# One gathered block's gates and indices made per pair of heads, and its gathers issued from the first pair on

## The chip, the cores and the metric

The program runs on one core of a Trainium2 chip. The metric is device time in microseconds of one execution of the whole program, as the median of a few runs. The engines of the core are TensorE (PE), VectorE (DVE), ScalarE (ACT), GpSimd (POOL) and SyncE (SP, which issues most loads here); 16 DMA engines move the data between memory and the on-chip buffers.

## The reference

One transformer block in float32: 512 tokens of width 2048 pass a mixer (an mLSTM branch and a forgetting attention), then a cross attention to a memory, then a PEER feed-forward, each followed by a layer norm of 2^0.25 x + h. The part that matters here is the feed-forward: for each token and each of 8 heads, two lists of 128 scores are cut to their best 16, the best 16 of the sums are kept, and the 8 x 16 = 128 experts that they name are read from two tables of 16384 rows.

```python
q = (x @ w_pq).reshape(B, S, PEER_HEADS, 2, PEER_DK // 2)
sc = jnp.einsum('bshpd,hpnd->bshpn', q, sub_keys)
top_s, top_i = lax.top_k(sc, PEER_TOPK)
cand_s = (top_s[..., 0, :, None] + top_s[..., 1, None, :]).reshape(B, S, PEER_HEADS, 256)
best_s, best_pos = lax.top_k(cand_s, PEER_TOPK)
idx = jnp.take_along_axis(cand_i, best_pos, -1)   # cand_i = first index * 128 + second index
g = jax.nn.softmax(best_s, -1)
# per token t: a[k] = expert_u[idx[k]] . x[t];  out = sum_k gelu(a[k]) * g[k] * expert_v[idx[k]]
```

## The kernel before

The 512 tokens are four blocks of 128. Blocks 0 and 1 do the feed-forward by gathering: 128 jobs per block fetch one row of `peer_u` for each of the 128 tokens (an indirect DMA from POOL into a 128 x 2048 tile `rows`, L1062), and DVE multiplies it with the tokens and sums (L1082, the "u product"); 128 more jobs fetch rows of `peer_v`, which DVE adds with their weights (L1098, the "v product"). The tile `rows` has three buffers. Blocks 2 and 3 do it densely: all 16384 experts are multiplied on PE, with weights from `uT` and `vD`.

Every PE product is made from split operands. A 1 MB weight tile (`raw`) is loaded by SP (L168), ACT writes its rounded part into a `ring` tile (two copies of 128 x 1024, L194), DVE writes the rest (L199, "the split"), and PE multiplies with both. There are two wide ring tiles in the second half of the program. Each split calls `tick`, which adds `rate * cost * mult` to a credit and issues one job for each whole credit; the product of a job is placed some ticks later (`lag`).

The program is written in the order of its Python code, and a list scheduler then orders the instructions of each engine. That order is fixed when the program runs.

The order of the second half is this. Block 0's jobs run under the mixer of tokens 128 to 511. When they are used up, residuals, cross attention and norms follow for block 1 (one block of tokens, `nb` = 1) and for blocks 2 and 3 (`nb` = 2), interleaved by hand. In this stretch lies the stage `pick1` (L1313 to L1339): `Choice.run` multiplies block 1 with `peer_wq` in four groups, one for each pair of heads; after each group `select` cuts the scores of that pair (`MAX`, `MAX_INDEX`, `MATCH_REPLACE` on DVE: 16-wide lists) and writes two index parts `i0`, `i1` and the best scores. Behind the fourth pair `soften` makes the gates of all heads at once, and `indices(1)` makes the row numbers `ei[1]` and copies the gates into `gg[1]`. Then `add_jobs(1)` puts block 1's 256 jobs on the list, with a rate of 256 jobs over 980 units and `mult` 0.65. The stages behind are `topk` (the choice for blocks 2 and 3, `mult` 0.65), `gbuild` (their weights as a dense matrix, 1.5), and the dense multiplication with `uT` and `vD` (0.86). Block 1's last v product is followed by its layer norm (`fin_gathered`) and, at the end, those of blocks 2 and 3 (`fin`).

Which buffers a weight load may use depends on the job list, too. `load_raw` (L160) counts the loads since the list was used up; from the seventh on, every second load goes into a `rows` buffer, of which three are then free. With jobs on the list that doesn't happen, and only the two `raw` buffers of the pool `w` are left in this part of the program:

```python
raws["idle"] = raws["idle"] + 1 if jobs and state["done"] >= len(jobs) else 0
if raws["idle"] > 6 and raws["n"] % 2:
    raw = rows_tile("raw")
else:
    p = raws["pools"][raws["n"] % len(raws["pools"])]
    raw = p.tile([P, 2048], F32, tag="raw", bufs=1 if p is raws.get("one") else 2, name=nm("raw"))
```

## Time and profile before

| what | value |
|---|---|
| median of 3 runs | 4523.76 us (4520.47 to 4525.49) |
| the profiled execution | 4524.7 us, span 4523.0 us, granted clock 0.992 |
| busy share of the span | PE 98%, DVE 83%, ACT 49%, POOL 20% |
| DMA | 1491.85 MB, mean 330 GB/s |
| L1062, `peer_u` and `peer_v` gathers | 256 and 256 |
| L1082 u products, L1098 v products | 256 of 2285 ns, 256 of 2347 ns |

The span is the time from the first to the last instruction; the execution's own time is 1.7 us more. A row of the window view gives, for a stretch of the span in us, the busy time of PE, of PE's weight loads (PEld), DVE, ACT and POOL with their instruction counts, then the granted PE clock, the DMA engines' busy share and GB/s. A row of the waits gives the engine and line that waited, what ended the wait, the sum in us, the number of waits and the longest. In a row of instruction groups stand line, engine, operation, output and inputs, count, busy us and mean ns, and the idle time ahead of the group. A DMA row gives count, KB and the median time from issue to landing.

### The profile page before, as it was taken

What the parts mean: (1) busy time and instruction counts of PE and PEld (TensorE: products, weight loads), DVE (VectorE), ACT (ScalarE), POOL (GpSimd) and SP (SyncE); (2) the same over time, 40 slices, a digit from 0 to 9 for tenths busy, and PEclk for the clock granted to TensorE, in tenths of its full rate; (3) what the DMA queues carried; (4) which work ended last, traced back from release to release, by engine and by line L of the source; (5) the groups of instructions that cost most, each with busy time, mean ns of one, the idle gap of its engine ahead of it and who ended that gap; (6) DMA issues with size and microseconds to landing.
All of it is one profiled execution on the core that took longest, in us unless ns stands there. A gap on an engine that the chain in (4) does not pass through costs nothing.

```text
span 4523.0 us, 65247 instructions
## 1 busy us (share of the span) xinstructions
PE 4414.1 (98%) x25702; PEld 3966.6 (88%) x25702; DVE 3739.9 (83%) x4326; ACT 2229.8 (49%) x3032; POOL 895.5 (20%) x631
## 2 busy tenths in 40 slices
PE   9999999999999999999999999898999999999998
PEld 8888888889888899999999778898998778999996
DVE  7877768657898977888878778899988999888888
ACT  6876776645344422333333586543773444434443
POOL 1000000000132222232222000111222223334242
PEclk9999999999999999999999999999999999999999
DMA  8899989766798889898889866786999999999997
GB/s 311 317 334 337 335 320 336 271 233 217 280 336 342 330 335 347 336 344 318 325 337 350 296 246 236 284 319 243 366 352 422 414 415 408 378 391 391 378 360 302
DMA packets 246325, 1491.85 MB, mean 330 GB/s; under 512 B 26845, under 2 KB 54557, under 8 KB 77697
## 3 DMA queue, kind: packets, MB, share of 16 engines
q1 hardware_dynamic: 151680, 890.60, 52.3%
q0 software_dynamic: 81664, 561.95, 31.7%
q10 hardware_dynamic: 12672, 35.13, 2.0%
q8 instruction: 201, 3.29, 0.3%
q14 instruction: 108, 0.88, 0.1%
HBM read 1426.72 MB, written 60.86 MB: 329 GB/s over the span
## 4 chain that ended last, share of the span: by engine, by line
PE 65%; DVE 5%; issue 4%; DMA 3%; ACT 1%; POOL 1%; DVEq 0%; ACTq 0%; SPq 0%; POOLq 0%
PE mm L220 22%; PE mm L270 6%; PE mm L263 6%; PE mm L262 6%; PE pa L1381 4%; PE mm L1530 4%; PE mm L1531 4%; PE mm L1527 4%; PE pa L1374 4%; PE pa L1377 4%; DVE ring L199 2%; DMA raw<-in_vD 1%; POOL rows L1062 1%; PE sm L638 1%; PE sm L716 1%
## 5 line engine op out<-in xcount | busy, mean ns | idle before, releaser
L194 ACT CAST ring<-raw 128x1024 fp32r<-128x1024 f32 x1568 | 1597.0, 1051 | 1456.0 <-PE mm L220 479.4
L199 DVE TENSOR_TENSOR ring<-raw,ring 128x2048 fp32r<-128x2048 f32 (+1 forms) x926 | 1813.4, 1961 | 530.0 <-ACT ring L194 268.0
L1062 POOL DMA_INDIRECT rows<-in_peer_u,ei x256 | 377.2, 1474 | 1593.0 <-DVE rows L1082 767.3
L220 PE MATMUL mm<-Ah,ring 128*128 128x384 f32 x2560 | 667.5, 339 | 1.7 <-ACT c L674 1.7
L1062 POOL DMA_INDIRECT rows<-in_peer_v,ei x256 | 451.5, 1764 | 938.0 <-DVE x2l L1098 635.1
L1098 DVE SCALAR_TENSOR_TENSOR x2l<-rows,dots,x2l 128x2048 f32<-128x2048 f32 x256 | 600.8, 2347 | 7.5 <-DMA rows<-in_peer_v,ei 7.1
L1082 DVE SCALAR_TENSOR_TENSOR rows<-rows,x2l 128x2048 f32<-128x2048 f32 x256 | 584.1, 2285 | 19.1 <-DMA rows<-in_peer_u,ei 18.9
L1374 PE MATMUL pa<-Xh,ring 128*128 128x256 f32 x2048 | 489.2, 282 | 2.9 <-ACT ring L194 2.9
L1377 PE MATMUL pa<-Xl,ring 128*128 128x256 f32 x2048 | 486.4, 280 | 0.0
L220 PEld LDWEIGHTS mm<-Ah,ring 128*128 128x128 f32 x2560 | 461.5, 188 | 7.6 <-ACT c L674 2.1
L220 PE MATMUL mm<-Al,ring 128*128 128x384 f32 x1280 | 427.0, 337 | 0.0
L1530 PE MATMUL mm<-ring,hph 128*128 128x512 f32 x1024 | 400.2, 393 | 9.0 <-ACT ring L194 6.8
L1531 PE MATMUL mm<-ring,hpl 128*128 128x512 f32 x1024 | 397.9, 390 | 0.0
L1374 PEld LDWEIGHTS pa<-Xh,ring 128*128 128x128 f32 x2048 | 387.5, 189 | 6.6 <-ACT ring L194 4.1
L1377 PEld LDWEIGHTS pa<-Xl,ring 128*128 128x128 f32 x2048 | 387.3, 189 | 2.4
L262 PE MATMUL mm<-ring,Zh 128*128 128x512 f32 x832 | 326.6, 393 | 3.3 <-ACT ring L194 3.3
L263 PE MATMUL mm<-ring,Zl 128*128 128x512 f32 x832 | 325.6, 391 | 0.0
L262 PE MATMUL mm<-ring,Ah 128*128 128x512 f32 x768 | 303.8, 396 | 1.1 <-ACT ring L194 1.1
L263 PE MATMUL mm<-ring,Al 128*128 128x512 f32 x768 | 300.5, 391 | 0.0
L1381 PE MATMUL pa<-Xh,ring 128*128 128x256 f32 x2048 | 264.4, 282 | 2.5 <-DVE ring L199 2.4
L220 PE MATMUL mm<-Bh,ring 128*128 128x384 f32 x1024 | 262.4, 339 | 3.2 <-ACT ring L194 2.5
L1527 PE MATMUL mm<-ring,hph 128*128 128x512 f32 x1024 | 254.4, 390 | 5.2 <-DVE ring L199 5.2
(395 smaller groups left out, 7042.7 us busy)
## 6 DMA issues: line engine op xcount, KB each, us to landing
raw<-in_w_in SPq DMA_DIRECT2D x256, 1024.0 KB, 6.7
raw<-in_uT SPq DMA_DIRECT2D x128, 1024.0 KB, 9.1
raw<-in_vD SPq DMA_DIRECT2D x128, 1024.0 KB, 9.5
raw<-in_w_out SPq DMA_DIRECT2D x48, 1024.0 KB, 6.1
raw<-in_peer_wq SPq DMA_DIRECT2D x48, 1024.0 KB, 5.2
raw<-in_w_xkv SPq DMA_DIRECT2D x32, 1024.0 KB, 6.5
raw<-in_w_br_ml SPq DMA_DIRECT2D x32, 1024.0 KB, 6.8
raw<-in_w_br_fx SPq DMA_DIRECT2D x32, 1024.0 KB, 7.4
```

What stands on the lines that cost most here:

```text
L194: x = nc.scalar.copy(hi[:, c:c + 1024], src[:, c:c + 1024])
L199: s = nc.vector.tensor_sub(lo, src, hi.bitcast(F32))
L220: i = nc.tensor.matmul(o, w, x, start=start and s % per == 0, stop=stop and s % per == per - 1)
L262: nc.tensor.matmul(banks[t], xh[:, tt], wh[:, c], start=k == 0, stop=False)
L263: nc.tensor.matmul(banks[t], xl[:, tt], wh[:, c], start=False, stop=False)
L1062: i = nc.gpsimd.indirect_dma_start(out=rows, out_offset=None, in_=I[table], in_offset=bass.IndirectOffsetOnAxis(ap=ei[t][:, k:k + 1], axis=0))
L1082: i = nc.vector.scalar_tensor_tensor(rows, rows, 1.0, tok[t]["x2l"], op0=ALU.mult, op1=ALU.mult, accum_out=d[:, k % GB:k % GB + 1])
L1098: i = nc.vector.scalar_tensor_tensor(acc, rows, d[:, GB + k % GB:GB + k % GB + 1], acc, op0=ALU.mult, op1=ALU.add)
L1374: i = nc.tensor.matmul(bank, uh[:, sl], xh, start=k == 0, stop=False)
L1377: nc.tensor.matmul(bank, uh[:, sl], xl, start=False, stop=False)
L1530: nc.tensor.matmul(banks[t][g], a[:, tt], vh[:, gs_], start=c == c0, stop=False)
L1531: nc.tensor.matmul(banks[t][g], b[:, tt], vh[:, gs_], start=False, stop=False)
```

## The change

`settle(g)` is new. It is called behind each `select` of `pick1`, and makes that pair's gates (exponential on ACT; sum, reciprocal and product on DVE, straight into `gg[1]`) and that pair's 32 row numbers (`ep[g]`, two DVE instructions), then appends the pair's 32 u jobs to the list. `soften` and `indices(1)` are not called for block 1 any more. The credit, a rate of 256 over 980, a lag of 2 and `mult` 0.6 are set ahead of `pick1`. `add_jobs(1)` appends the 128 v jobs alone; it no longer resets the credit. The `mult` of the dense stage goes from 0.86 to 0.81. Order and number of the 256 gathers of the block are the same.

```diff
+            def settle(self, g):
+                sl = slice(32 * g, 32 * g + 32)
+                e = self.gates[:, 0, sl]
+                ev = e.rearrange("p (h k) -> p h k", k=16)
+                sm = self.tp.tile([P, 2], F32, tag="s", bufs=2, name=nm("s"))
+                nc.scalar.activation(e, e, AF.Exp)
+                nc.vector.tensor_reduce(out=sm, in_=ev, axis=AX.X, op=ALU.add)
+                nc.vector.reciprocal(sm, sm)
+                nc.vector.tensor_tensor(gg[1][:, sl].rearrange("p (h k) -> p h k", k=16), ev,
+                                        sm.unsqueeze(2).to_broadcast([P, 2, 16]), op=ALU.mult)
+                ef = self.tp.tile([P, 32], F32, tag="ef", bufs=2, name=nm("ef"))
+                nc.vector.scalar_tensor_tensor(ef, self.sel["i0"][0][:, sl], float(PKEYS), self.sel["i1"][0][:, sl],
+                                               op0=ALU.mult, op1=ALU.add)
+                nc.vector.tensor_copy(ep[g], ef)
+                jobs.extend((job_u, 1, k) for k in range(32 * g, 32 * g + 32))
...
                         self.select(t, 2 * g, sc)
-                self.soften()
+                        if settle:
+                            self.settle(g)
+                if not settle:
+                    self.soften()
...
-                                             in_offset=bass.IndirectOffsetOnAxis(ap=ei[t][:, k:k + 1], axis=0))
+                                             in_offset=bass.IndirectOffsetOnAxis(
+                                                 ap=ep[k // 32][:, k % 32:k % 32 + 1] if t else ei[0][:, k:k + 1], axis=0))
...
-            jobs.extend((f, t, k) for f in (job_u, job_v) for k in range(NC_))
+            jobs.extend((f, t, k) for f in (job_u, job_v)[t:] for k in range(NC_))
...
             c = Choice(pp, pp, 1)
-            cr = c.run(X2b, nc.sync)
+            state["lag"], state["rate"], state["credit"], state["mult"] = 2, 2 * NC_ / 980.0, 0.0, 0.6
+            cr = c.run(X2b, nc.sync, True)
...
-            c.indices(1)
...
         add_jobs(1)
-        state["lag"] = 2
-        set_rate(980.0)
         state["mult"] = 0.65
...
-        state["mult"] = 0.86
+        state["mult"] = 0.81
```

The scheduler's order changes with it. Line numbers of the changed program are its own: L169 is the load, L200 the split, L1104 the u product, L1120 the v product; the instructions of `select` stand one line lower. Numbers in names tell tiles of the same kind apart. The first place is SP's queue around the load of the second pair's weights. Before:

```order
L168 DMA raw_21665<-in_peer_wq 128x2048
L168 DMA raw_21830<-in_peer_wq 128x2048
L168 DMA raw_21735<-Ad 128x2048
L168 DMA raw_21864<-in_peer_wq 128x2048
L168 DMA raw_21847<-in_peer_wq 128x2048
L168 DMA raw_21914<-Ad 128x2048
L1012 DMA keysT_21628<-in_keysT 128x512
L1012 DMA keysT_21827<-in_keysT 128x512
L1069 DMA x2l_22923<-x2d 128x2048
L168 DMA raw_21881<-in_peer_wq 128x2048
```

Now:

```order
L169 DMA raw_21668<-in_peer_wq 128x2048
L169 DMA raw_21738<-Ad 128x2048
L169 DMA raw_21841<-in_peer_wq 128x2048
L1030 DMA keysT_21631<-in_keysT 128x512
L1030 DMA keysT_21838<-in_keysT 128x512
L1091 DMA x2l_21846<-x2d 128x2048
L169 DMA raw_21864<-in_peer_wq 128x2048
L169 DMA raw_21881<-in_peer_wq 128x2048
L169 DMA raw_21901<-in_peer_wq 128x2048
L1030 DMA keysT_22036<-in_keysT 128x512
```

Before, three of the second pair's four weight loads stood ahead of the two key loads and the block's `x2l` load; now one does, and three stand behind them.

The second place is DVE from the split with which the last of the cross attention's `Ad` tiles is taken (the 14th split counted from the one at 2717.10 us of the profile). Before:

```order
L199 TENSOR_TENSOR ring_149<-raw_22122,ring_149 128x2048
L946 MATCH_REPLACE rep_21959<-v_21943,sc_21912 128x128
L946 MATCH_REPLACE rep_21965<-v_21943,sc_21912 128x128
L982 SCALAR_TENSOR_TENSOR pp_21811<-pf_21813,pp_21811 128x32
L989 TENSOR_TENSOR eq_21818<-eq_21818,ixf_21790 128x512
L199 TENSOR_TENSOR ring_19990<-raw_22196,ring_19990 128x2048
L947 MAX v_21943<-rep_21959 128x8
L947 MAX v_21943<-rep_21965 128x8
L983 TENSOR_TENSOR pf_21813<-pp_21811 128x32
L990 TENSOR_REDUCE sel_i_2363_21625<-eq_21818 128x32
```

Now:

```order
L200 TENSOR_TENSOR ring_152<-raw_22158,ring_152 128x2048
L977 TENSOR_SCALAR pos_21997<-pos_21997 128x32 x2
L1014 TENSOR_REDUCE s_22028<-sel_g_21630 128x2
L1104 SCALAR_TENSOR_TENSOR rows_21848,dots_21886<-rows_21848,x2l_21846 128x2048
L979 CAST pp_22012<-pos_21997 128x96
L1015 RECIPROCAL s_22028<-s_22028 128x2
L1104 SCALAR_TENSOR_TENSOR rows_21850,dots_21886<-rows_21850,x2l_21846 128x2048
L981 SCALAR_TENSOR_TENSOR pf_22014<-pp_22012 128x32
L1016 TENSOR_TENSOR gg_147<-sel_g_21630,s_22028 128x32
L942 MAX v_22264<-sc_22125 128x8 x4
L1104 SCALAR_TENSOR_TENSOR rows_21939,dots_21886<-rows_21939,x2l_21846 128x2048
```

At the same split the first pair's selection was still under way before; now it is finished, the second pair's is at its end (32 more DVE instructions stand ahead of this split than before), and the first three u products of block 1 stand directly behind the split. Twelve u products stand between it and the 27th split, where before none did; from there until the split at 3775 us of the profile the changed order is 12 to 15 products ahead of the old one at the same split. In the 66 splits from 3388 to 3775 us the old order holds 66 products and the new one 65; behind them the lead falls from 14 to two or three at the end.

The third place is DVE at the end of the program. Before, the block's last v product and the statistics and first half of its layer norm stood behind the last split, and the second half stood among the last norms of blocks 2 and 3. Now:

```order
L200 TENSOR_TENSOR ring_152<-raw_37362,ring_152 128x2048
L1120 SCALAR_TENSOR_TENSOR x2l_21846<-rows_37273,dots_30439,x2l_21846 128x2048
L1150 BN_STATS fst_37420<-x2l_21846 128x6 x4
L1151 BN_AGGR fst_37420<-fst_37420 128x2
L1132 SCALAR_TENSOR_TENSOR x2l_21846<-x2l_21846,fst_37420,lw_37358 128x1024 x2
L287 TENSOR_SCALAR fst_37420<-fst_37420 128x1
L200 TENSOR_TENSOR ring_19993<-raw_37391,ring_19993 128x2048
L289 RECIPROCAL fst_37420<-fst_37420 128x1
```

The norm's first half now stands ahead of the last but one split, and its second half ahead of the last one.

More of the change, by code (lines that the diff above doesn't have):

```diff
@@ L133, in build @@
         iota = cp.tile([P, P], F32, tag="iota", name="iota")
-        ei = [cp.tile([P, P], I32, tag=f"ei{t}", name=f"ei{t}") for t in range(2)]
+        ei = [cp.tile([P, P], I32, tag="ei0", name="ei0")]
         nc.gpsimd.iota(ei[0], pattern=[[1, P]], base=0, channel_multiplier=0)
@@ L150, in build @@
         gg = [cp.tile([P, P], F32, tag=f"gg{t}", name=f"gg{t}") for t in range(2)]
+        ep = [cp.tile([P, 32], I32, tag=f"ep{g}", name=f"ep{g}") for g in range(4)]
         ticks = []
@@ L1004, in soften, with run @@
                 nc.vector.tensor_tensor(e, e, sm.unsqueeze(2).to_broadcast([P, 8 * nb, 16]), op=ALU.mult)
-            def run(self, X2, ld):
+            def settle(self, g):
[13 more added lines that the diff above has]
+                jobs.extend((job_u, 1, k) for k in range(32 * g, 32 * g + 32))
+            def run(self, X2, ld, settle=False):
                 tp, nb = self.tp, self.nb
@@ L1314, in build @@
             c = Choice(pp, pp, 1)
-            cr = c.run(X2b, nc.sync)
+            if state["done"] < len(jobs):
+                raise RuntimeError(f"{len(jobs) - state['done']} jobs left")
+            state["lag"], state["rate"], state["credit"], state["mult"] = 2, 2 * NC_ / 980.0, 0.0, 0.6
+            cr = c.run(X2b, nc.sync, True)
             for i in range(15):
@@ L1338, in build @@
             next(cr, 0)
-            c.indices(1)
         pre = ExitStack()
         pp = pre.enter_context(pool("pre", side="right"))
-        while state["done"] < len(jobs):
-            raise RuntimeError(f"{len(jobs) - state['done']} jobs left")
         add_jobs(1)
-        state["lag"] = 2
-        set_rate(980.0)
         state["mult"] = 0.65
```

## The prediction

> **What bounds the kernel now.** I read the page's head, then the windows by stage, then who waits in the stretch that the change touches.
>
> ```profile
> span 4523.0 us, 65247 instructions
> PE 4414.1 (98%) x25702; PEld 3966.6 (88%) x25702; DVE 3739.9 (83%) x4326; ACT 2229.8 (49%) x3032; POOL 895.5 (20%) x631
> ```
>
> TensorE is busy nearly everywhere, so the question for each stage is how much PE idles there, and for whom. The windows of the stages behind `pick1`:
>
> ```profile
> 2880.00:3120.00 240.00, 239.12 (x2032) 238.71 (x2031) 228.48 (x524) 101.33 (x116) 40.35 (x29) 1.00 0.83 320
> 3160.00:3420.00 260.00, 252.41 (x2127) 249.11 (x2125) 234.10 (x239) 183.06 (x453) 66.81 (x40) 0.99 0.93 365
> 3420.00:3785.00 365.00, 351.30 (x1617) 285.17 (x1616) 339.04 (x288) 145.51 (x169) 98.31 (x64) 1.00 1.01 415
> 3785.00:4455.00 670.00, 667.65 (x4286) 608.12 (x4285) 584.57 (x326) 274.65 (x303) 251.32 (x116) 1.00 0.96 382
> ```
>
> From 3785 us on, where the change has about 12 gathers fewer, PE is busy 667.65 of 670 us: no more than 2.35 us can be won there. From 3420 to 3785 us the DMA engines are full (share 1.01), PE idles 13.7 us, and that is where fewer gathers would help; but the order places 66 products in those 66 splits before and 65 now. From 2880 to 3120 us PE is busy 239.12 of 240, so whatever is late at 2880 stays late.
>
> Now `pick1` and the norm behind it, from the 1st to the 14th split after 2717 us, to the 27th, and to the next stage's first split:
>
> ```profile
> 2717.00:2768.70 51.70, 49.67 (x228) 40.38 (x227) 43.52 (x97) 37.13 (x50) 0.00 (x0) 0.97 0.83 311
> 2768.70:2836.00 67.30, 62.92 (x286) 51.43 (x284) 65.89 (x160) 31.67 (x43) 0.00 (x0) 1.00 0.42 149
> 2836.00:2867.30 31.30, 22.95 (x136) 18.87 (x137) 22.53 (x86) 24.00 (x44) 0.00 (x0) 0.78 0.44 156
> 2717.00:2867.30 150.30, 135.54 (x648) 110.68 (x647) 131.95 (x341) 92.80 (x136) 0.00 (x0) 0.94 0.56 206
> ```
>
> POOL does nothing here and the DMA engines are at 0.56, which is what the change means to use. But in the middle stretch DVE is busy 65.89 of 67.30 us. DVE is the bound there, and PE follows it: PE loses 4.4 us in the middle and 8.4 behind. What DVE waits for in its idle 8.2, 1.4 and 8.8 us:
>
> ```profile
> DVE ring L199 <- ACT ring L194: 9.5, 6, 3.1
> DVE v L941 <- ACT sc L1040: 6.1, 2, 5.5
> DVE ring L199 <- PE mm L220: 5.5, 2, 3.4
> ```
>
> The 5.5 us wait is the last stretch's: the fourth pair's scores, which nothing but PE and ACT can hurry.
>
> **The change part by part.** The costs per instruction, from the groups:
>
> ```profile
> L1082 DVE SCALAR_TENSOR_TENSOR rows<-rows,x2l 128x2048 f32<-128x2048 f32 x256 | 584.1, 2285 | 19.1 <-DMA rows<-in_peer_u,ei 18.9
> L976 DVE TENSOR_SCALAR pos<-pos 128x32 uint32<-128x32 uint32 x8 | 1.0, 173 | 0.0
> L199 DVE TENSOR_TENSOR ring<-raw,ring 128x2048 fp32r<-128x2048 f32 x27 | 61.7, 2286 | 9.8 <-ACT ring L194 8.3 <-PE mm L270 1.5
> L194 ACT CAST ring<-raw 128x1024 fp32r<-128x1024 f32 x55 | 55.7, 1053 | 43.6 <-DVE ring L199 20.7 <-PE mm L263 19.2 <-DVE xst L861 2.5
> ```
>
> *Moved and added DVE work.* By the order twelve u products now stand between the 14th and the 27th split: 12 x 2.285 = 27.4 us. `settle` makes 4 x 5 DVE instructions in place of six, 14 more; the nearest row is one of 32 wide at 173 ns: 2.4 us. Together 29.8 us. The old idle can take in some of it. The order puts 32 more of the short selection instructions (0.17 to 0.29 us, some 8 us) ahead of the 14th split, where 8.2 us are idle. So the middle holds 65.89 + 29.8 - 8 = 87.7 us of work against 67.30 us before: +20.4 us even if DVE there never waits. The last stretch keeps its wait for the scores, which comes behind the moved products: 0. The floor, with all 18.35 us of idle filled, is 29.8 - 18.35 = +11.4 us; the ceiling, with none filled, +29.8.
>
> *Buffers for the loads.* With jobs on the list from the first `settle` on, `load_raw` stops giving out `rows` tiles. So the weight loads fall from five buffers (two of `w`, three of `rows`) to two, just where the matrices for one block take a new tile every few us. SP's queue shows it: two more of the second pair's weights now queue behind the key and `x2l` loads.
>
> ```profile
> raw<-in_peer_wq SPq DMA_DIRECT2D x18, 1024.0 KB, 5.5
> raw<-in_w_in SPq DMA_DIRECT2D x93, 1024.0 KB, 7.1
> 2733.74 2.29 DVE L199 TENSOR_TENSOR ring<-raw,ring 128x2048 fp32r<-128x2048 f32 x1 [0.22 <-PE mm L270]
> 2768.71 2.29 DVE L199 TENSOR_TENSOR ring<-raw,ring 128x2048 fp32r<-128x2048 f32 x1
> ```
>
> One buffer's round is the landing (5.5 us here; 7.1 in the stage at 1300 to 2400 us, which runs gathers with two buffers), two ACT copies (2.1) and the split (2.3): 9.9 to 11.5 us, so two buffers give a split each 4.95 to 5.75 us. Between the two quoted splits lie nine intervals in 35.0 us. At 4.95 they take 44.6, at 5.75 51.8: +9.6 to +16.8 us, and the 8 us of earlier selection fit inside. I take +11, near the row of this stretch. The low end is 0, if the loads are asked for early enough. In the middle, 13 intervals in some 88 us are 6.7 us each, over the 4.95: the loads bind only where two splits stand close.
>
> *Gathers that land late.* DVE runs in order, so a product whose rows have not landed holds up the splits queued behind it, and PE waits for those.
>
> ```profile
> rows<-in_peer_u,ei POOLq DMA_INDIRECT x71, 9.8
> 3906.04 2.75 POOL L1062 DMA_INDIRECT rows<-in_peer_v,ei  x1 [4.96 <-DVE x2l L1098]
> 3911.11 1.14 POOL L1062 DMA_INDIRECT rows<-in_peer_v,ei  x1 [2.32 <-DVE x2l L1098]
> ```
>
> In the next stage (2880 to 3420 us) a gather lands 9.8 us after its issue. By the order some two dozen short instructions and two splits, about 9 us, lie between the first pair's row numbers and the first product, and three gathers of 1 MB start together there. I take +5 us for this and for close splits in the middle, from 0 (all hidden) to 18 (a 1.5 us wait at each of twelve products). The Trainium skill's page "DMA: Bandwidth & Descriptors", section "Anatomy of one DMA — SWDGE (gpsimd) path", gives a DMA from POOL about 2.0 us plus its bytes over 436 GB/s, an estimated 4.4 us for 1 MB; by that every gather would be hidden and the sum 5 us less. The 9.8 us of the row are more than twice that.
>
> *Behind `pick1`.* Between 3160 and 3388 us the lead grows from 12 to 15, three more products and 3 MB where the DMA share is 0.93: 0 to 3 x 2.285 = 6.9 us; I take 2, as DVE still idles 26 us in that window. The lower `mult` has no price.
>
> *The end.*
>
> ```profile
> 4499.42 1.97 PE L1527 MATMUL mm<-ring,hph 128*128 128x512 f32 x8
> 4511.15 2.48 DVE L1113 SCALAR_TENSOR_TENSOR x2l<-x2l,fst,lw 128x1024 f32<-128x1024 f32 x2
> ```
>
> PE's last product ends at 4501.4; behind it DVE alone sets the end. The second half of the gathered block's norm, 2.48 us, now stands ahead of the last split: -2.5 us, from -5 (with its small steps) to +3 (if it makes the last splits late).
>
> **Sum** on the profiled execution's 4524.7 us (0.9 over the median, nothing here): 11 + 20.4 + 5 + 2 - 2.5 = +35.9, so **4561 us**.
>
> **The rivals.** *VectorE alone:* the loads are asked for early and gathers land in time; then the first stretch costs nothing: 20.4 + 2 - 2.5 = +19.9, 4545 us. For it: DMA share 0.56. Against it: five buffers become two. *The idle absorbs it:* every idle us of DVE is filled, +11.4 - 2.5, 4534 us. Against it: 8.8 of the 18.35 us lie behind the last moved product. *Not slower:* the relief at the end pays. Place: 3785 to 4455 us. Price: 12 gathers of 1.05 MB at the 382 GB/s of that window, 33 us, which would give 4561 - 33 = 4528, and 4501 together with the floor. It decides if PE waits for gathers or loads there, and the window's 2.35 us of idle speak against it. *Gathers that start slowly:* in the dense stage, where DVE is nearly full, a gather takes POOL 2.75 us in one row and 1.14 in the next. If each of the twelve starts 1.6 us late with DVE full and DVE waits for each, that is +19 more: 4580 us. Beside it stands a rule of the Trainium skill, page "SBUF — State Buffer", section "Who interferes with whom": a VectorE instruction with two inputs in that memory blocks a GpSimd instruction that reads it, and the splits and products are such. The two lengths in the trace fit it; against a price POOL's idle 150 us speak, since a late start only counts if the landing does. *That the change does not do what it says,* the order excludes: the products stand where the text puts them.
>
> **How the numbers follow.** A measurement here tells about 0.2% (9 us) from no change. Forecast 0.50; VectorE alone 0.25; slow gathers 0.10; absorbed 0.08; relief at the end 0.07. The range is 4533 to 4586: down to the absorbed case, and up to the sum with the loads at 16.8 and the gathers at 18 (4580), plus 6 of the 10 us that the growing lead (4.9) and the end (5.5) could add at their worst. Faster by over 0.2% needs the relief together with the floor: 0.05. Within 0.2%: 0.02 of the relief and 0.05 of the absorbed case, whose 4534 lies on the edge: 0.07. Slower: the rest, 0.88.
>
> **What would show it.** In the profile after: `rows` products from about 2780 us on; the 14th split some 11 us later, the 27th some 36 us later; DVE busy nearly all of the time between them; weight loads that are issued only when a split has freed a buffer, and DVE waits for L194's line that end in a `raw` landing; PE idle of 40 us or more in this stretch; from there the same stages shifted by one amount, and an end some 2 us shorter. If the 27th split comes at its old time, the reckoning of DVE's work is wrong; if the shift is 20, that of the buffers; if the dense stage from 3785 us is shorter by more than 3 us, that of the end.

## The result, and the profile after

The changed kernel takes 4557.84 us in the median of four runs (4550.52 to 4564.33), the kernel before 4523.74 beside it: a ratio of 1.0076, 95% interval 1.0064 to 1.0088. It is slower by 34.1 us, where 37 were forecast. The profiled execution took 4558.29 us. The head of its page:

```profile
span 4556.6 us, 65269 instructions
PE 4421.1 (97%) x25702; PEld 3966.0 (87%) x25702; DVE 3741.9 (82%) x4340; ACT 2231.2 (49%) x3037; POOL 884.3 (19%) x631
```

VectorE's busy time grew by 2.0 us and PE's by 7.0, with the same number of matmuls; the rest of the 33.6 us by which the span grew is waiting. Work was moved, hardly any added. Where the time lies is read by cutting both executions at the same splits: the 1st, 14th and 27th of the prediction, the next stage's first, and the 16th from the end. The windows of before, with the row that sums the three of `pick1` and the norm, then the two behind:

```profile
sum 150.18, PE 135.42 PEld 110.56 DVE 131.92 ACT 92.67 POOL 0.00; mean PE 45.14 PEld 36.85 DVE 43.97 ACT 30.89 POOL 0.00
...
2867.27:4408.30 1541.03, 1499.59 (x10047) 1374.54 (x10046) 1393.79 (x1478) 705.06 (x1054) 450.02 (x243) 0.99 0.93 372
4408.30:4523.00 114.70, 92.06 (x469) 78.19 (x467) 100.71 (x89) 34.47 (x38) 30.12 (x13) 0.93 0.77 302
```

And of after, at the same splits (the cuts of a run lie up to 0.4 us ahead of its splits, all by the same amount, 0.16 us here; so the differences between cuts hold, and "the end" is that much too long):

```profile
2720.12:2783.66 63.54, 54.36 (x232) 40.82 (x231) 51.41 (x138) 35.35 (x50) 4.26 (x3) 0.95 0.66 240
2783.66:2873.14 89.48, 67.87 (x282) 53.05 (x280) 85.60 (x158) 36.19 (x50) 13.52 (x11) 0.91 0.77 286
2873.14:2904.33 31.19, 22.73 (x131) 18.68 (x132) 22.17 (x85) 23.74 (x43) 0.00 (x0) 0.72 0.52 182
sum 184.21, PE 144.96 PEld 112.55 DVE 159.17 ACT 95.28 POOL 17.79; mean PE 48.32 PEld 37.52 DVE 53.06 ACT 31.76 POOL 5.93
...
2904.33:4442.04 1537.71, 1494.01 (x10054) 1372.20 (x10053) 1374.76 (x1456) 704.55 (x1054) 432.37 (x233) 0.99 0.92 366
4442.04:4556.60 114.56, 92.37 (x465) 77.54 (x463) 94.69 (x85) 34.13 (x38) 21.08 (x11) 0.94 0.71 279
```

The first split comes at 2720.28 us instead of 2717.10: 3.2 us that this execution had lost by then; executions differ by as much (in e5 below, the same program, it comes at 2713.7). Then the first stretch grows by 11.9 us (51.61 in the kernel before, from its 2717.09 to 2768.70), the middle by 22.1 (67.36 before), the last by nothing: `pick1` takes 184.2 us instead of 150.2, 34.0 more. Behind it 3.3 us are won, at the end no more than 0.3. In the middle stretch VectorE is busy 85.60 of 89.48 us, as before it was 65.9 of 67.4: it is still the bound, with 19.7 us more to do; 2.5 us more of idle make up the 22.1.

Who waits in `pick1`, on VectorE and then on TensorE:

```profile
DVE ring L200 <- ACT ring L195: 13.1, 8, 6.5
DVE v L942 <- ACT sc L1058: 5.5, 1, 5.5
...
DVE rows L1104 <- DMA rows<-in_peer_u,ep: 2.6, 2, 2.0
```

```profile
PE mm L271 <- DVE ring L200: 17.1, 6, 11.0
PE mm L263 <- ACT ring L195: 12.0, 7, 5.6
```

These rows are of 2715 to 2905 us. The splits' wait for ACT's copy alone tells little: in the kernel before it is 8.3 us within the stretch (the 9.5 quoted in the prediction are of 2707 to 2880 us). What ACT's copies themselves wait for has changed. Before (2717 to 2867 us), then after (2720 to 2904 us):

```profile
ACT ring L194 <- DVE ring L199: 20.7, 5, 7.2
ACT ring L194 <- PE mm L263: 19.2, 15, 6.0
```

```profile
ACT ring L195 <- DMA raw<-in_peer_wq: 31.1, 10, 6.3
ACT ring L195 <- DMA raw<-Bd: 22.4, 6, 10.2
```

Before, ACT waited for VectorE and PE, and for weight tiles to land 1.0 us in all; now it waits 59.8 us for landings (the third row, of `Ad`, is 6.3): the loads bind. The wait for the fourth pair's scores is the old 5.5 us, to the tenth. Only two products waited for their gathers, 2.6 us together, but what stood behind them waited too. PE waits 17.1 us for splits, 11.0 of it for the 27th alone, which VectorE, with its queue of selection and products, reaches only at 2873. On SP's queue, in time order with start and length:

```profile
2722.60 0.33 SPq L169 DMA_DIRECT2D raw<-in_peer_wq  x1
2729.05 0.80 SPq L1030 DMA_DIRECT2D keysT<-in_keysT  x2
2729.95 0.38 SPq L1091 DMA_DIRECT2D x2l<-x2d  x1
2731.61 0.33 SPq L169 DMA_DIRECT2D raw<-in_peer_wq  x1
```

For 9 us after 2722.60 no weight tile is asked for; in the kernel before, five are asked for from 2719.42 to 2736.07, never more than 5.4 us apart. The tile asked for at 2731.61 holds up the split that needs it:

```profile
2742.04 2.29 DVE L200 TENSOR_TENSOR ring<-raw,ring 128x2048 fp32r<-128x2048 f32 x1 [6.51 <-ACT ring L195]
```

It starts 8.8 us after the split ahead of it, where before it was 2.5.

### The profile page after: what moved, and what is told of

Same layout as the page of the kernel before. It is cut to its first block, busy times and chain, and to the rows that moved or that the text cites. A ratio compares the mean times of both kernels' runs of the same rounds, so it can differ in the third digit from the quotient of the medians.

```text
span 4556.6 us, 65269 instructions
## 1 busy us (share of the span) xinstructions
PE 4421.1 (97%) x25702; PEld 3966.0 (87%) x25702; DVE 3741.9 (82%) x4340; ACT 2231.2 (49%) x3037; POOL 884.3 (19%) x631
## 4 chain that ended last, share of the span: by engine, by line
PE 57%; DMA 7%; DVE 6%; issue 6%; ACT 2%; POOL 1%; DVEq 0%; ACTq 0%; SPq 0%; POOLq 0%
PE mm L221 22%; PE mm L271 5%; PE mm L264 5%; PE mm L263 5%; DMA rows<-in_peer_v,ep 3%; PE pa L1401 3%; PE pa L1394 3%; PE pa L1397 3%; DVE ring L200 2%; PE mm L1547 2%; PE mm L1550 2%; PE mm L1551 2%; DMA raw<-in_vD 1%; POOL rows L1083 1%; ACT ring L195 1%
## 5 line engine op out<-in xcount | busy, mean ns | idle before, releaser
L200 DVE TENSOR_TENSOR ring<-raw,ring 128x2048 fp32r<-128x2048 f32 (+1 forms) x926 | 1811.2, 1960 | 552.8 <-ACT ring L195 286.1
L1120 DVE SCALAR_TENSOR_TENSOR x2l<-rows,dots,x2l 128x2048 f32<-128x2048 f32 x256 | 600.4, 2345 | 21.7 <-DMA rows<-in_peer_v,ep 18.4
L1104 DVE SCALAR_TENSOR_TENSOR rows<-rows,x2l 128x2048 f32<-128x2048 f32 x256 | 583.4, 2283 | 13.6 <-DMA rows<-in_peer_u,ei 7.7
L1394 PE MATMUL pa<-Xh,ring 128*128 128x256 f32 x2048 | 489.0, 282 | 5.1 <-ACT ring L195 5.0
L1550 PE MATMUL mm<-ring,hph 128*128 128x512 f32 x1024 | 399.9, 392 | 7.5 <-ACT ring L195 5.7
L1083 POOL DMA_INDIRECT rows<-in_peer_u,ep x128 | 192.2, 1501 | 1036.4 <-DVE rows L1104 401.3
L1083 POOL DMA_INDIRECT rows<-in_peer_v,ep x128 | 279.1, 2180 | 539.0 <-DVE x2l L1120 299.0
L1083 POOL DMA_INDIRECT rows<-in_peer_u,ei x128 | 173.2, 1353 | 516.6 <-DVE rows L1104 316.1
L1083 POOL DMA_INDIRECT rows<-in_peer_v,ei x128 | 173.1, 1353 | 474.1 <-DVE x2l L1120 261.1
```

The costliest lines, as they stand in the source:

```text
L200: s = nc.vector.tensor_sub(lo, src, hi.bitcast(F32))
L1083: i = nc.gpsimd.indirect_dma_start(out=rows, out_offset=None, in_=I[table], in_offset=bass.IndirectOffsetOnAxis(ap=ep[k // 32][:, k % 32:k ...
L1104: i = nc.vector.scalar_tensor_tensor(rows, rows, 1.0, tok[t]["x2l"], op0=ALU.mult, op1=ALU.mult, accum_out=d[:, k % GB:k % GB + 1])
L1120: i = nc.vector.scalar_tensor_tensor(acc, rows, d[:, GB + k % GB:GB + k % GB + 1], acc, op0=ALU.mult, op1=ALU.add)
L1394: i = nc.tensor.matmul(bank, uh[:, sl], xh, start=k == 0, stop=False)
L1550: nc.tensor.matmul(banks[t][g], a[:, tt], vh[:, gs_], start=c == c0, stop=False)
```

## The experiments

Each kernel ran beside the kernel before on one chip; "the stretch" is `pick1` from the first split to the next stage's first, 150.2 us in the kernel before. In four runs that move no products, gathers or buffers in it (e6, e8, e9, e11) it takes 150.0 to 150.5, and in the three profiles of the changed kernel's own order (after, e5, e10) 184.2 to 185.7; so a difference of 2 us is seen there, while whole executions of the kernel before lay up to 24 us apart (4510.67 to 4534.77, beside e1). All of it in one table; "behind" runs from the next stage's first split to the 16th from the end, "end" from there to the last instruction, all from the profiled executions:

| run | stretch | against before | behind | end | ratio of the times (95%) |
|---|---|---|---|---|---|
| before | 150.2 | | 1541.0 | 114.7 | |
| after | 184.2 | +34.0 | 1537.7 | 114.6 | 1.0076 (1.0064 to 1.0088) |
| e1: two load buffers alone | 159.7 | +9.5 | 1533.9 | 115.0 | 1.0020 (1.0007 to 1.0033) |
| e2: after, no products | 169.6 | +19.4 | 1551.8 | 114.9 | 1.0081 (1.0060 to 1.0103) |
| e3: after, no gathers | 179.8 | +29.6 | 1550.9 | 118.1 | 1.0094 (1.0071 to 1.0118) |
| e4: after, three buffers | 174.0 | (17 late at its start) | 1550.7 | 116.2 | 1.0115 (1.0094 to 1.0137) |
| e5: after again | 185.7 | +35.5 | 1538.3 | 116.1 | 1.0079 (1.0064 to 1.0093) |
| e6: settle alone | 150.5 | +0.3 | 1546.3 | 115.2 | 1.0020 (1.0010 to 1.0030) |
| e7: products alone | 170.2 | +20.0 | 1538.2 | 116.3 | 1.0055 (1.0040 to 1.0069) |
| e8: before, 0.94 | 150.0 | -0.2 | 1543.6 | 128.8 | 1.0046 (1.0033 to 1.0059) |
| e9: before, 0.90 | 150.0 | -0.2 | 1544.2 | 112.9 | 1.0000 (0.9991 to 1.0009) |
| e10: after, 0.86 | 184.4 | +34.2 | 1544.3 | 108.2 | 1.0053 (1.0038 to 1.0069) |
| e11: before, 12 gathers fewer | 150.4 | +0.2 | 1535.8 | 109.1 | 0.9985 (0.9975 to 0.9994) |
| e12: after, half the rate | 171.7 | +21.5 | 1552.2 | 114.7 | 1.0070 (1.0054 to 1.0085) |

**e1, two load buffers alone.** The kernel before, with

```diff
-            raws["idle"] = raws["idle"] + 1 if jobs and state["done"] >= len(jobs) else 0
+            raws["idle"] = raws["idle"] + 1 if jobs and not raws.get("hold") and state["done"] >= len(jobs) else 0
...
                         self.select(t, 2 * g, sc)
+                        raws["hold"] = nb == 1 and not self.lean
...
         add_jobs(1)
+        raws["hold"] = False
```

> The kernel before, with one thing changed: from the first selection of pick1 on, the weight loads get no rows tiles, so two buffers instead of five; no settle, no earlier gathers. My theory (the loads' two buffers cost the first stretch its 12 us, VectorE's moved products the middle its 22): the 14th split comes 10 to 13 us later than in the kernel before, the 27th split keeps that shift or gives up to 5 us of it back, since VectorE without the moved products has little idle there; time about 4534 (4529 to 4537), 7 to 13 over the kernel before. Rival (the loads are asked for early enough, and the first stretch became longer through settle and the new order of the selection): 14th split within 3 us of its old time, time 4522 to 4527.

The three windows of its stretch:

```profile
2714.45:2778.81 64.36, 55.08 (x230) 42.05 (x229) 51.31 (x135) 35.30 (x48) 0.00 (x0) 0.92 0.63 221
2778.81:2847.50 68.69, 64.38 (x287) 51.92 (x285) 60.97 (x127) 36.12 (x49) 0.00 (x0) 1.00 0.55 198
2847.50:2874.17 26.67, 20.94 (x132) 17.77 (x133) 20.61 (x81) 20.89 (x40) 0.00 (x0) 0.82 0.53 191
```

The first stretch is 12.7 us longer, with no product, no gather and no settle in it: the two buffers make the whole of the 11.9 us. The middle adds 1.3, the last gives 4.5 back. 9.5 us remain, and the time, 9 us over the kernel before (3 to 15), fits. The rival fell. The scheduler's order changed with the buffers, too: VectorE has 135 instructions in the first stretch, where it had 97. So e1 prices the two buffers together with the order that they bring.

**e2, the products' arithmetic left out.** The changed kernel, with

```diff
-                i = nc.vector.scalar_tensor_tensor(rows, rows, 1.0, tok[t]["x2l"], op0=ALU.mult, op1=ALU.mult,
-                                                   accum_out=d[:, k % GB:k % GB + 1])
+                if t == 1 and k < 12:
+                    i = nc.vector.tensor_copy(d[:, k % GB:k % GB + 1], rows[:, 0:1])
+                else:
+                    i = nc.vector.scalar_tensor_tensor(rows, rows, 1.0, tok[t]["x2l"], op0=ALU.mult, op1=ALU.mult,
+                                                       accum_out=d[:, k % GB:k % GB + 1])
```

> The changed kernel, whose first twelve u products are each replaced by a copy of one column (128x1) out of the gathered rows: the gathers, their landing waits, settle and the two load buffers stay; the arithmetic of twelve products is left out. My theory: the middle stretch loses VectorE's 27 us of products and its excess falls from 22 to between 0 and 4 us, the first stretch keeps its 12; time about 4536 (4532 to 4541), 17 to 25 under the changed kernel. Rival (gathers and their traffic are what makes the middle long, by late landings or by slower weight loads): the middle keeps at least 10 of its 22 us, time 4545 or more.

It missed, and both signs of the rival are there: the middle keeps 12.9 of its 22.1 us, and the time is 4558.8 us. The stretch lost 15 us, and the time did not fall at all. The middle window, the sum, and VectorE's waits in the stretch:

```profile
2780.22:2860.46 80.24, 66.38 (x286) 52.64 (x284) 63.45 (x150) 37.41 (x53) 8.79 (x10) 0.95 0.80 314
...
sum 169.55, PE 140.60 PEld 110.27 DVE 135.18 ACT 93.63 POOL 14.04; mean PE 46.87 PEld 36.76 DVE 45.06 ACT 31.21 POOL 4.68
```

```profile
DVE ring L200 <- ACT ring L195: 17.4, 13, 6.5
DVE dots L1105 <- DMA rows<-in_peer_u,ep: 3.7, 2, 2.9
```

VectorE is idle 17 us of the middle now, and the splits and copies wait for loads and gathers, 17.4 and 3.7 us in the stretch. Without the products' time in which they can land, the gathers cost 9.8 us over e1. Slower weight loads are a small part of it: a tile of `peer_wq` lands 5.2 us after its issue here, 4.9 in e1 (medians); a gather lands after 7.5. So products and gathers overlap: when the products are left out, the gathers take up part of the time that was freed (e3 leaves out the gathers instead). That the total stayed is another matter: "behind" takes 10.8 us longer than in the kernel before (see e5).

**e3, the gathers left out.** The changed kernel, with

```diff
-            rows = gather("peer_u", t, k, s)
+            rows = rows_tile("rows") if t == 1 and k < 12 else gather("peer_u", t, k, s)
...
-                i = nc.vector.scalar_tensor_tensor(rows, rows, 1.0, tok[t]["x2l"], op0=ALU.mult, op1=ALU.mult,
+                i = nc.vector.scalar_tensor_tensor(rows, tok[t]["x2l"] if t == 1 and k < 12 else rows, 1.0, tok[t]["x2l"], op0=ALU.mult, op1=ALU.mult,
```

> The changed kernel without the first twelve gathers: their products read the tokens' own tile x2l twice instead, at VectorE's same cost, and wait for no transfer; those twelve dot products are not the reference's. My theory: the gathers' part is small (1 to 5 us), because VectorE's time for the products and the two load buffers set the pace: the 27th split still comes 28 to 36 us later than in the kernel before, time 4551 to 4558. Rival (slow or late gathers make the stretch long): the shift at the 27th split falls to 20 us or less, time 4542 or less.

```profile
2782.10:2865.26 83.16, 68.02 (x293) 54.27 (x291) 82.51 (x181) 36.41 (x49) 2.74 (x1) 0.93 0.46 165
...
sum 179.80, PE 146.47 PEld 113.84 DVE 158.67 ACT 95.81 POOL 2.74; mean PE 48.82 PEld 37.95 DVE 52.89 ACT 31.94 POOL 0.91
```

The stretch is 29.6 us longer than before (at the 27th split 29.7, inside the 28 to 36), with VectorE busy 82.51 of 83.16 us in the middle: the products and the buffers make most of the loss without the twelve gathers. The order is another one here: four of the twelve products stand in the first stretch. Beside these products the gathers add 4.4 (after) to 5.9 us (e5). The time again lies higher than expected, by the part behind.

**e4, a third load buffer.** The changed kernel, with

```diff
-        with pool("pick1") as pp:
+        with pool("rx") as rx, pool("pick1") as pp:
+            raws["pools"], raws["one"] = [wp, rx, wp], rx
...
+            raws["pools"] = [wp]
...
-                        t = tp.tile([P, 512], F32, tag="qT", bufs=3 - self.lean, name=nm("qT"))
+                        t = tp.tile([P, 512], F32, tag="qT", bufs=3 - (nb == 1), name=nm("qT"))
```

> The changed kernel with a third buffer for the weight loads in pick1 and the norm behind it (8 KB per partition, paid for by one qT buffer fewer in the selection). My theory: with three buffers the loads no longer bind the first stretch; the 14th split comes within 4 us of its time in the kernel before and the total falls by 7 to 12 us, to about 4548 (4545 to 4551); the middle keeps its 20 to 24 us of excess. Rival (the loads were not the bound; VectorE's added work in total is, and only moves about): the 27th split keeps its 34 us, time 4555 or more.

```profile
2731.65:2779.79 48.14, 48.14 (x228) 40.27 (x227) 41.24 (x91) 30.80 (x36) 0.00 (x0) 0.99 0.72 267
2779.79:2873.95 94.16, 71.07 (x290) 55.69 (x288) 93.61 (x201) 36.64 (x50) 15.40 (x13) 0.86 0.77 280
```

No answer on the total. The first stretch falls to 48.14 us, below the kernel before, with PE busy all of it, as the theory has it. But this is no clean test: its first split is already 17 us late (14.6, and this execution was 2.3 ahead): the new rotation of buffers leaves SP without a load to issue from 2691 to 2720 us, and PE waits 8.8 us for one copy. And what left the first stretch came back in the middle, where VectorE is busy 93.61 of 94.16 us. The kernel is slower than the changed one, so the expected time missed. By the letter the rival's two signs are there (the 27th split 38 us late, 4574 us), but with such a start they decide nothing, either.

**e5, the changed kernel again.** No edit.

> The changed kernel itself, beside the others on one chip. In e2, e3 and e4 the profiles lost some 7 to 10 us more between 3330 and 3600 us, where the DMA engines are full, which the first profile of the changed kernel did not. Theory (that stage moves by some us from one execution to the next, with the same program): this profile shows a shift there of its own size, between -5 and +10 us against the first one, and at the next stage's first split behind pick1 the same 34 us (33 to 35) as the first. Rival (the first profile is what the changed kernel always does, and the other three lost more by their order): the shift from 2900 to 4440 us is again between 0 and -4 us. Time by either 1.006 to 1.010 of the kernel before.

The stretch takes 185.7 us (+35.5), "behind" 1538.3 against 1537.7 in the first profile: the rival was right. So execution alone does not explain the 10 us that e2, e3, e4 lost there; their order is the likely cause. The list scheduler orders VectorE's instructions anew, far behind an edit: e3 and e4 have one and the same VectorE order from 3150 to 3600 us, another than the changed kernel's, and take 1550.9 and 1550.7 us behind. Three kernels with the VectorE order of the kernel before in that part (e7 and e11 exactly, e1 nearly) take 1533.9 to 1538.2 us to its 1541.0: some 7 us, by which one order varies by itself. (e8 and e9 have that order there, too, but another rate behind it.)

**e6, settle alone.** The changed kernel, with

```diff
-                jobs.extend((job_u, 1, k) for k in range(32 * g, 32 * g + 32))
...
-            state["lag"], state["rate"], state["credit"], state["mult"] = 2, 2 * NC_ / 980.0, 0.0, 0.6
...
-            jobs.extend((f, t, k) for f in (job_u, job_v)[t:] for k in range(NC_))
+            jobs.extend((f, t, k) for f in (job_u, job_v) for k in range(NC_))
...
         add_jobs(1)
+        state["lag"] = 2
+        set_rate(980.0)
...
-        state["mult"] = 0.81
+        state["mult"] = 0.86
```

> The changed kernel with settle making gates and row numbers per pair, but with all 256 jobs appended where the kernel before appends them, with its rates and its dense stage's 0.86: so the loads keep five buffers and no product or gather is moved. My theory (settle's small instructions are worth nothing): the 14th, the 27th and the next stage's first split within 3 us of their times in the kernel before, time within 0.15% of it. Rival (the exponential on ACT and the waits of settle's chain per pair cost VectorE and ACT time between the splits): next stage's first split 5 us later or more, ratio 1.0015 or more.

```profile
sum 150.52, PE 135.64 PEld 110.45 DVE 132.47 ACT 92.98 POOL 0.00; mean PE 45.21 PEld 36.82 DVE 44.16 ACT 30.99 POOL 0.00
```

Settle costs 0.3 us. Yet the time is 0.20% up over nine runs, as the rival had it, and not where the rival put it: in the profile 5.2 us come behind, which is less than the 7 us by which one order varies. What PE waits for from 3150 to 3570 us in e6, in the stage that builds the dense weights, then the row of before for the same wait:

```profile
PE mm L1466 <- ACT o L1465: 14.4, 8, 6.2
```

```profile
PE mm L1446 <- ACT o L1445: 4.7, 8, 1.7
```

**e7, products alone.** The kernel before, with five load buffers and no gathers:

```diff
-        with pool("pick1") as pp:
+        with pool("jk") as jk, pool("pick1") as pp:
+            junk = jk.tile([P, 1536], F32, tag="junk", name="junk")
+            nc.vector.memset(junk, 1.0)
+            todo = [0, 0]
+            def spare(s, cost):
+                todo[0] += 1
+                if todo[0] > 12 and todo[1] < 16:
+                    todo[1] += 1
+                    i = nc.vector.scalar_tensor_tensor(junk, junk, 1.0, junk, op0=ALU.mult, op1=ALU.mult)
+                    after(i, s)
+            ticks.append(spare)
...
+            ticks.remove(spare)
```

> The kernel before with VectorE work alone added in pick1: 16 products of 128x1536 on a tile of their own (about 27 us in all by their width, what twelve u products take), ten of them or more between the 14th and the 27th split; no gathers, and the loads keep five buffers. My theory (VectorE is the bound of the middle stretch, whatever the buffers): the next stage's first split comes 14 to 22 us later, ratio 1.003 to 1.005. Rival (the products cost much only together with two load buffers, since with five the loads run ahead and the old idle takes the products in): 10 us later or less, ratio 1.0022 or less.

The added group, and the windows:

```profile
L1322 DVE SCALAR_TENSOR_TENSOR junk<-junk 128x1536 f32<-128x1536 f32 x16 | 27.9, 1745 | 0.0
```

```profile
2772.54:2856.65 84.11, 66.19 (x275) 50.83 (x273) 84.11 (x176) 30.59 (x41) 0.00 (x0) 0.95 0.32 117
...
sum 170.21, PE 140.40 PEld 111.20 DVE 158.99 ACT 92.51 POOL 0.00; mean PE 46.80 PEld 37.07 DVE 53.00 ACT 30.84 POOL 0.00
```

27.9 us of VectorE work (twelve of the sixteen products in the middle) cost 20.0 us of time, with every buffer there and the DMA engines at 0.32; VectorE is busy 84.11 of 84.11 us. The theory holds; the ratio, 1.0055, is a little above its 1.003 to 1.005. And e1's 9.5 and e7's 20.0 make 29.5, e3's 29.6: these two terms add.

**e8 and e9, the end alone.** The kernel before, with one number:

```diff
-        state["mult"] = 0.86
+        state["mult"] = 0.94
```

and 0.90 in e9.

> The kernel before with one number changed, the dense stage's mult 0.94 instead of 0.86: its gathers run somewhat faster, the last v product and all of that block's norm stand ahead of the last eleven splits instead of behind them, and nothing in pick1 changes. My theory (what the changed kernel wanted at its end can be had without moving gathers into pick1): the tail behind PE's last product falls by 3 to 8 us, the dense stage stays as long as it is, ratio 0.9982 to 0.9995. Rival (faster gathers make the splits of the dense stage late, where the DMA engines are at 0.96): the tail falls, but PE idles as much or more ahead of it, ratio 1.000 or more.

> The kernel before with the dense stage's mult 0.90 instead of 0.86. The last v product comes four splits ahead of the end instead of behind the last split, one product per split as ever (0.94 had put five products and the first part of the norm between two splits), and the norm of that block lies between the last splits. My theory (e8 lost its 17 us only at that heap): the tail behind PE's last product falls by 5 to 9 us, the last splits come 0 to 6 us late, ratio 0.998 to 1.000. Rival (a faster rate itself costs, by gathers that make splits of the dense stage late): shift of 3 us or more before split 910, ratio 1.002 or more.

PE's longest wait between 4400 and 4500 us in e8, then the end of e9:

```profile
PE mm L1530 <- ACT ring L194: 19.7, 1, 19.7
```

```profile
4413.23:4526.10 112.87, 91.31 (x452) 75.95 (x450) 92.77 (x85) 33.91 (x38) 17.96 (x9) 0.93 0.68 272
```

e8 missed, and its rival's ratio is there: the tail behind PE's last product falls from 21.6 to 17.2 us, as expected, but five v products and four statistics stand in one heap ahead of a split, and PE waits 19.7 us once for what stands behind the heap. In e9 there is no heap: the tail falls by 3.1 us (5 to 9 were expected), the end is some 2 us shorter, "behind" 3.2 longer, the time the same. The rival's shift is there, its 1.002 is not. So neither beats the kernel before.

**e10, the changed kernel with its old dense rate.**

```diff
-        state["mult"] = 0.81
+        state["mult"] = 0.86
```

> The changed kernel with the dense stage's mult as it was before, 0.86 instead of 0.81: block 1's last v product and norm come some nine splits earlier; pick1 is the same. My theory (with 0.81 the norm stands ahead of the last splits and makes them 9 to 11 us late, which eats what the shorter tail wins): the last splits are late by less than 4 us, the short tail stays, and the time falls by 5 to 10 us against the changed kernel, ratio 1.0055 to 1.007. Rival (the end is not worth anything either way, or the faster rate costs as much in the dense stage): ratio 1.0075 or more.

```profile
4448.49:4556.70 108.21, 89.96 (x451) 76.04 (x449) 72.95 (x76) 36.58 (x40) 3.33 (x1) 0.93 0.51 197
```

The end falls to 108.2 us, 6 to 8 under the changed kernel's: with 0.86 the norm of the gathered block is over before the last five splits. But the cut flatters it: the 30 splits ahead of it take 169.6 us, 164.8 in both profiles of the changed kernel. From there to the end it is 277.7 us against 279.2 and 280.7, so 1.5 to 3 us are won net. The ratio, 1.0053 against 1.0076 and 1.0079, is just under the expected 1.0055 to 1.007, though the intervals overlap; the profiled execution, the slowest of the four, does not show where the rest is won.

**e11, twelve gathers fewer.** The kernel before, with

```diff
+            if t == 1 and k >= NC_ - 12:
+                return lambda s2: None
             rows = gather("peer_v", t, k, s)
```

> The kernel before without the last twelve of block 1's v gathers and their products (they are left out, so that block's output lacks twelve experts): what the dense stage and the end win when twelve gathers fewer fall into them, at no cost in pick1. My theory: no more than 3 us between 3785 and 4440 us, and 3 to 9 us at the end, since that block's norm moves under PE; ratio 0.9975 to 0.9993. Rival (relief at the end: the dense stage waits for its transfers): 12 x 1.05 MB at 382 GB/s, 33 us or at least half of it, ratio 0.996 or less.

```profile
4399.26:4508.40 109.14, 91.93 (x470) 78.49 (x469) 75.18 (x77) 34.54 (x38) 2.74 (x1) 0.94 0.53 205
```

The end is 5.6 us shorter. From the split at 3775.01 us of the kernel before to the 16th from the end it takes 633.4 us, before 633.3: twelve gathers fewer in the dense stage are worth nothing there. The rival's 33 us are excluded.

**e12, half the rate.** The changed kernel, with

```diff
-            state["lag"], state["rate"], state["credit"], state["mult"] = 2, 2 * NC_ / 980.0, 0.0, 0.6
+            state["lag"], state["rate"], state["credit"], state["mult"] = 2, 2 * NC_ / 980.0, 0.0, 0.3
...
-        state["mult"] = 0.81
+        state["mult"] = 0.84
```

> The changed kernel with half the rate in pick1 (mult 0.3 instead of 0.6), so that six gathers and products of block 1 stand there instead of twelve, and 0.84 in the dense stage so that the list comes to its end; two load buffers as in the changed kernel. My theory (buffers 9.5 us, products in proportion, gathers 4): next stage's first split 20 to 25 us later than in the kernel before, against 34 with twelve; ratio 1.004 to 1.006. Rival (the first products go into VectorE's idle time and only the later ones cost): 9 to 17 us later, ratio 1.0035 or less.

```profile
sum 171.71, PE 145.60 PEld 113.20 DVE 146.84 ACT 92.19 POOL 9.94; mean PE 48.53 PEld 37.73 DVE 48.95 ACT 30.73 POOL 3.31
```

The stretch is 21.5 us longer, in the 20 to 25: the products cost about in proportion from the first on, beside the fixed price of the buffers. The ratio, 1.0070, is over the expected 1.004 to 1.006, and its part behind, 1552.2, has the excess.

## Why the prediction was right

**The middle's work, +20.4.** Right: VectorE's work between the two splits grew from 65.95 to 85.60 us, 19.7 (87.7 were reckoned), and e7 prices VectorE's work alone at 20.0. The reason given, that VectorE is the bound there and PE follows, is shown by e7, where nothing else was added.

**The load buffers, +11.** Right in its mechanism, as e1 shows: 11.9 in the first stretch, 12.7 in e1 alone, of which 9.5 are left at the stretch's end. In its size it was in part luck. The nine intervals that it priced at 4.95 to 5.75 us took 4.64 each (41.8 us), 4.73 in e1: less than the least of them, since the tiles of `peer_wq` landed in 4.9 us in e1, not in 5.5; with that the same reckoning gives 4.65. They make +6.8 of the 11.9; another 6.3 are the one split ahead of them that started 8.8 us after its forerunner, which the sum did not price. That the buffers fall from five to two is nowhere in the diff; it was found in `load_raw`'s counter, and on SP's queue.

**Gathers landing late, +5.** Right in size as it was put, on top of the other two: 4.4 to 5.9 (after and e5 against e3, whose order differs). But the term is no property of the gathers: without the products it is 9.8 (e2), so about half of it is hidden in the products' own time. The prediction took terms as if each stood alone, and e2's expectation failed by that. By the Trainium skill's page "DMA: Bandwidth & Descriptors", section "Anatomy of one DMA — SWDGE (gpsimd) path", from which the estimate of 4.4 us came, the term would have been nothing; the runs speak against it: in e2 a gather landed 7.5 us after its issue, in the median of thirteen.

**Behind, +2.** Not seen: -3.3 and -2.8 in the two profiles. The three products more under busy DMA engines cost nothing that shows, but one order varies by 7 us there, so a term of 2 us could not be told either way. Another order took 10 to 11 us more in e2, e3, e4 and e12: most likely a cause that the prediction didn't have, and that is larger than its term.

**The end, -2.5.** Wrong for the whole end: about nothing in the first profile, some +1.3 in e5. The tail behind PE's last product did become 3.1 us shorter (21.6 to 18.5), as forecast. The norm ahead of the last splits shortens the tail, but holds the splits up, as the profile of after shows:

```profile
4520.42 2.35 DVE L1120 SCALAR_TENSOR_TENSOR x2l<-rows,dots,x2l 128x2048 f32<-128x2048 f32 x1 [4.08 <-DMA rows<-in_peer_v,ep]
...
4525.61 2.48 DVE L1132 SCALAR_TENSOR_TENSOR x2l<-x2l,fst,lw 128x1024 f32<-128x1024 f32 x2
...
4528.07 2.28 DVE L200 TENSOR_TENSOR ring<-raw,ring 128x2048 fp32r<-128x2048 f32 x1
...
4533.63 2.29 DVE L200 TENSOR_TENSOR ring<-raw,ring 128x2048 fp32r<-128x2048 f32 x1
```

The last v product waits 4.08 us for its gather, the norm follows it, and the last split starts at 4533.63, 42.7 us later than before, where the 16th from the end was 33.9 later. The prediction named this (+3, "if it makes the last splits late") and took the other end. The lower `mult` "has no price", it said: by e10 the last 15 splits and the tail take 6 to 8 us longer with it, most of which the 30 splits ahead of them give back; what it costs in all stays open: 1.5 to 3 us by the profiles, more by the ratios, whose intervals overlap.

**The sum.** On the profiled execution +35.9 were forecast and 33.6 came. The parts were less near: the stretch 36.4 against 34.0, behind +2 against -3.3, the end -2.5 against about -0.3, and 3.2 us by which this execution was late from the start. That the small terms cancelled to within 3 us is luck; that the stretch holds the loss, and why, is not.

**The signs.** Counted from the first split, the 14th came 11.9 us later than before and the 27th 34.0 ("some 11" and "some 36" were named). PE idled 39.2 us in the stretch, where "40 us or more" stood. The dense stage was not shorter: 634.8 us from the split at 3775 us of the kernel before to the 16th from the end, 633.3 before.

**The rivals.** *VectorE alone* fell with e1. *The idle absorbs it* fell with e7 and e12: 27.9 us cost 20.0, and half the products still cost. *Relief at the end* fell with e11. *Slow gathers*, at +19 more, fell with e3, where all that the gathers cost is 4.4 to 5.9 us, and with the trace: the row of the first gathers' durations, least, median and longest in ns:

```profile
L1083 POOL DMA_INDIRECT rows<-in_peer_u,ep x13: 932/934/2955, 2778.8 to 2869.9; - x13
```

Beside a VectorE that was busy 85.60 of 89.48 us the median gather took 0.93 us on POOL. The blocking that the Trainium skill's page "SBUF — State Buffer", section "Who interferes with whom", describes is not contradicted by the longest, 2955 ns, but it did not hold here for most of the gathers.

**What stays open.** Why e2, e3, e4 and e12 lose 10 us behind the stretch was not shown. Only for e6's smaller loss was a wait read (PE waits for ACT's scaled rows); that the order is the cause is argued, from one profile of each kernel. A third load buffer without the new rotation that spoiled e4 was not run.

## What to carry to other kernels

Idle DMA engines and an idle GpSimd say nothing if the work that follows the transfer belongs to an engine that is full in that stage: read the stage's window, not the average. When work is moved into a stage, look up what its presence switches off; here a job list that isn't empty took three of five load buffers. And where a scheduler orders the program anew, price an edit in its own stretch, between two fixed instructions: that was steady to 1.5 us here for one program, while the rest moved by 10.

## What the runs showed of the hardware

The granted PE clock fell where PE had to wait, and PE's own work became longer. For the stretch's matmuls PE was busy 135.42 us in the kernel before, 140.40 in e1 and in e7, 144.96 in the changed kernel; the granted clock of the middle was 1.00 in the kernel before and 0.91 in the changed one. So some 9.5 of the 34 us show as longer matmuls, not as waits (busy time is modelled there).

The wait comes first, as windows of PE alone show around the longest one, the 11.0 us for the 27th split (PE busy and its matmuls, granted clock, DMA share, GB/s):

```profile
2864.60:2866.80 2.20, 0.04 (x1) 1.00 0.78 328
2866.90:2875.60 8.70, 0.00 (x0) 0.50 0.36 121
2875.60:2883.90 8.30, 6.91 (x25) 0.50 0.00 0
```

The clock is halved 2.2 us after PE fell idle, and stays so for 8.3 us after it went on. It need not be a long wait: the clock fell six times in the changed kernel's stretch, and in the 3.41 us ahead of each fall PE was busy 1.68, 1.49, 0.00, 0.73, 1.19 and 1.71 us. So several short waits can do it, where PE is busy for no more than half of such a stretch (by the modelled ends). Cutting the whole profile in steps of 3.41 us from these falls on bears this out: of 1303 stretches behind which the clock stayed full, all but one have PE busy for 1.73 us or more. The Trainium skill's page "TensorE: Matmul & The Clock Gate", section "Part 1: The HAM clock gate (the "warmup" mystery)", says that the clock falls to half after at least one idle window of some 3.4 us. The trace agrees with the half and with the length, but the windows ahead of the falls were not idle throughout.
